# Strassen's seven products for four of eleven K-tile pairs of a down projection, in a float32 decoder layer

## The chip, the cores and the metric

The kernel runs on one core of a Trainium2 chip. The metric is device time in microseconds (us) of one execution, the median of several runs. TensorE (PE in the profile, PEld for its weight loads) multiplies matrices into PSUM banks; VectorE (DVE) and ScalarE (ACT) work elementwise and can read PSUM; GpSimd (POOL) works elementwise from SBUF; SyncE (SP) mostly issues DMA transfers. A tile lies on 128 partitions; "128x1024" is partitions by elements of each.

## The reference

A decoder layer in float32 on x of 256 tokens by 2048 features: two kinds of attention with one input and one output projection, then a channel mixer. Only the channel mixer is touched:

```python
h = rmsnorm(x, pre_ffn_g[l])
u = causal_dwconv(h @ w_up[l], conv_w[l], conv_b[l])      # 2048 -> 2 * 5632, width 3
gate, val = jnp.split(u, 2, axis=-1)
y = (jax.nn.gelu(gate, approximate=True) * val) @ w_down[l]   # 5632 -> 2048
x = x + rmsnorm(y, post_ffn_g[l])
```

## The kernel before

**Numbers.** Each float32 operand is split into a high part of a format that TensorE multiplies fast (fp32r in the profile) and a low part, the rest. A product is the sum of three matmuls: high by high, high by low, low by high. ScalarE makes the high part (a copy that rounds), VectorE the low part (operand minus high part). For weights these are the lines L111 and L114 (`w_split`), for activations L311 and L312 (`split`).

**Weights.** `w_load` (L68) lets SP's queue bring 512 KB of weights into a tile `raw` (128x1024); `raw` is a ring of five, so a load waits until the tile five loads earlier has been read by its low part. High and low parts, `whi` and `wlo`, are rings of five too.

**The channel mixer** runs in two halves of the 5632 features. In each half eleven steps g make two tiles each of `G`, the activated features: 22 tiles of 128 features by 256 tokens, each as high part (columns 0 to 255) and low part (256 to 511). One step multiplies the normalised input hT (16 K tiles, high and low) by 256 gate columns and 256 value columns of w_up (`proj_T4`, L283 for high weights, L289 for low ones). Each result goes through `conv`: ScalarE copies the cross term out of PSUM (`cs`, L879), VectorE adds (`u`, L880), GpSimd multiplies by the token scales (L881), ScalarE makes the first tap (L883), VectorE the other two (L885, L887). Then gate times value (L958) and the split into `G`. Banks of PSUM come from two tags, "acc" and "att", four of each; steps g take turns between them, from "acc" in both halves.

**The down projection** of a half follows its eleven steps: G (22 K tiles) by w_down, in passes of 512 output columns (n = 0 to 3). A pass has eleven pairs of K tiles; a pair is one load of two K tiles by 512 columns, and 2 K tiles x 2 token tiles x 3 = 12 matmuls of 128x512 (`mm3`, L308), added up in two PSUM banks. In half 0 ScalarE copies the result to `y_sb`; in half 1 `down` adds PSUM to `y_sb` (L972), squares and sums for the norm (L973) and multiplies by the gain (GpSimd, with the gain tile `gbf`). Half 1's last pass (n = 3) is written out separately: it keeps the last parts in the memory of hT (`rest`), and finishes with the residual `x_sb` and the output transfers.

**Order.** TensorE's order is the program's. The other engines' orders come from a scheduler, except where the program fixes them (the first gate step up to `order.__exit__`, and the finish). What an engine does next is fixed when the kernel is built; at run time each instruction waits for its operands.

## Time and profile before

| | |
|---|---|
| median of 3 runs | 1077.66 us (1077.61 to 1078.52) |
| profiled execution: span | 1076.3 us |
| TensorE busy | 1064.1 us (99%) |
| VectorE, ScalarE, GpSimd busy | 744.6, 611.2, 219.7 us (69%, 57%, 20%) |
| read from memory | 199.58 MB, 187 GB/s over the span |
| up projection, half 0, to its last up matmul | until 584.90 us |
| down projection, half 0 | 584.90 to 704.58 |
| up projection, half 1 | 704.58 to 947.02 |
| down projection, half 1, to its last pass's wait | 947.02 to 1067.66 |

The span is that of one profiled execution, 1.4 us under the median of the runs. The stage limits are ends of pieces in the chain of waits (the chain of work that ended last, followed back). In rows of the profile, "L308" is a line of the kernel, "x528" a count, and what follows "|" is the busy time of a group, the mean of one in ns, and the idle time before them with what ended it. Where a row begins with two numbers, they are its start in us and its length. A row of a table of windows has a window, its length, and for PE, PEld, DVE, ACT and POOL the busy time with the count in brackets; then the granted TensorE clock (1.00 is full), the DMA engines' busy share, and GB/s.

### The profile page before, as it was taken

Reading aid. Unit: us, or ns where it says so; the run is one execution under the profiler, and the core shown is the slowest. Engines: PE = TensorE matmul, PEld = TensorE weight load, DVE = VectorE, ACT = ScalarE, POOL = GpSimd, SP = SyncE. Lnnn points to the kernel's source line nnn. Section 1 sums busy time; section 2 is a strip of 40 time slices with the busy share of each in tenths; the row PEclk is TensorE's granted clock in tenths of the full one; section 3 lists DMA queues with packets and bytes.
Section 4 is the critical chain, followed back from the end, with each engine's and each line's share of the span. In section 5 each row is a group of like instructions: output and inputs, shape, how many; then the busy total and the mean of one; then the engine's idle time right before and its main releaser. Section 6 shows DMA issues by size and latency. Waiting matters only on the chain.

```text
span 1076.3 us, 16248 instructions
## 1 busy us (share of the span) xinstructions
PE 1064.1 (99%) x5986; PEld 926.8 (86%) x5986; DVE 744.6 (69%) x1200; ACT 611.2 (57%) x1060; POOL 219.7 (20%) x252
## 2 busy tenths in 40 slices
PE   9999999999999999999999999999999999999996
PEld 7889988887889888888888888888888888888886
DVE  5988877887577876777777444457777777765563
ACT  6766766666556765655555443446555555644450
POOL 4243343332022121212122000002121221201111
PEclk9999999999999999999999999999999999999999
DMA  8635556555873666656565666666565666666652
GB/s 282 209 119 176 183 155 210 158 161 157 298 235 105 216 214 193 189 186 197 186 190 193 196 197 193 195 193 190 184 197 188 189 193 193 193 192 197 193 167 79
DMA packets 164970, 202.88 MB, mean 188 GB/s; under 512 B 6780, under 2 KB 130972, under 8 KB 164380
## 3 DMA queue, kind: packets, MB, share of 16 engines
q1 hardware_dynamic: 164176, 201.27, 59.0%
q8 instruction: 47, 0.77, 0.3%
q10 hardware_dynamic: 716, 0.58, 0.2%
q14 instruction: 31, 0.25, 0.1%
HBM read 199.58 MB, written 2.11 MB: 187 GB/s over the span
## 4 chain that ended last, share of the span: by engine, by line
PE 93%; DVE 2%; DMA 1%; POOL 1%; ACT 1%; issue 1%; SPq 0%; DVEq 0%; POOLq 0%; ACTq 0%
PE bank_acc L308 34%; PE bank_acc L283 16%; PE bank_att L283 14%; PE bank_acc L289 8%; PE bank_att L289 7%; PE bank_acc L252 5%; PE bank_acc L257 3%; DVE wlo L114 1%; PE bank_att L474 1%; PE bank_att L509 1%; PE bank_acc L914 1%; PE bank_acc L910 0%; PE bank_att L220 0%; POOL scr L441 0%; PE bank_att L533 0%
## 5 line engine op out<-in xcount | busy, mean ns | idle before, releaser
L114 DVE TENSOR_TENSOR wlo<-raw,whi 128x1024 fp32r<-128x1024 f32 (+3 forms) x357 | 438.4, 1236 | 239.6 <-ACT whi L111 235.6
L111 ACT CAST whi<-raw 128x1024 fp32r<-128x1024 f32 (+3 forms) x356 | 363.8, 1035 | 258.6 <-issue 123.7
L308 PE MATMUL bank_acc<-whi,G 128*128 128x512 f32 (+1 forms) x724 | 214.4, 378 | 0.0
L881 POOL TENSOR_TENSOR u<-u,rowf 128x256 f32<-128x256 f32 x88 | 95.7, 1108 | 496.9 <-DVE u L880 493.4
L283 PE MATMUL bank_acc<-hT,whi 128*128 128x512 f32 x736 | 173.3, 390 | 0.0
L283 PEld LDWEIGHTS bank_acc<-hT,whi 128*128 128x128 f32 x736 | 136.4, 188 | 27.4
L308 PEld LDWEIGHTS bank_acc<-whi,G 128*128 128x128 f32 x724 | 133.7, 188 | 25.5
L283 PE MATMUL bank_att<-hT,whi 128*128 128x512 f32 x640 | 150.6, 390 | 0.0
L283 PEld LDWEIGHTS bank_att<-hT,whi 128*128 128x128 f32 x640 | 118.7, 188 | 23.9
L308 PE MATMUL bank_acc<-wlo,G 128*128 128x512 f32 (+1 forms) x362 | 137.0, 379 | 0.0
L289 PEld LDWEIGHTS bank_acc<-hT,wlo 128*128 128x128 f32 x736 | 89.3, 188 | 2.0
L289 PE MATMUL bank_acc<-hT,wlo 128*128 128x256 f32 x736 | 89.8, 279 | 0.0
L252 PE MATMUL bank_acc<-hT,whi 128*128 128x512 f32 x352 | 89.2, 396 | 0.0
L308 PE MATMUL bank_acc<-whi,oT 128*128 128x512 f32 (+1 forms) x272 | 82.5, 380 | 0.0
L308 PEld LDWEIGHTS bank_acc<-wlo,G 128*128 128x128 f32 x362 | 68.1, 188 | 12.9
L289 PEld LDWEIGHTS bank_att<-hT,wlo 128*128 128x128 f32 x640 | 77.6, 188 | 1.7
L289 PE MATMUL bank_att<-hT,wlo 128*128 128x256 f32 x640 | 77.9, 279 | 0.0
L252 PEld LDWEIGHTS bank_acc<-hT,whi 128*128 128x128 f32 x352 | 63.0, 188 | 11.3
L308 PEld LDWEIGHTS bank_acc<-whi,oT 128*128 128x128 f32 x272 | 50.2, 188 | 9.3
L308 PE MATMUL bank_acc<-wlo,oT 128*128 128x512 f32 (+1 forms) x136 | 51.3, 377 | 0.0
L308 PE MATMUL bank_acc<-whi,hT 128*128 128x384 f32 (+1 forms) x192 | 47.5, 324 | 0.0
L257 PE MATMUL bank_acc<-hT,wlo 128*128 128x256 f32 x352 | 47.5, 282 | 0.0
(204 smaller groups left out, 1140.4 us busy)
## 6 DMA issues: line engine op xcount, KB each, us to landing
raw<-in_w_up_dram SPq DMA_DIRECT2D x176, 512.0 KB, 3.7
raw<-in_w_down_dram SPq DMA_DIRECT2D x88, 512.0 KB, 4.6
raw<-in_w_in_dram SPq DMA_DIRECT2D x51, 512.0 KB, 3.5
raw<-in_w_out_dram SPq DMA_DIRECT2D x32, 512.0 KB, 4.7
raw<-in_w_in_dram SPq DMA_DIRECT2D x16, 384.0 KB, 3.3
cb<-c_dram SPq DMA_DIRECT2D x8, 256.0 KB, 3.5
x_sb<-in_x_dram SPq DMA_DIRECT2D x2, 1024.0 KB
raw<-in_w_in_dram SPq DMA_DIRECT2D x5, 408.0 KB, 3.2
```

Source lines behind the costliest of these rows:

```text
L111: i1 = act.copy(hi[:, cs], raw[:, cs])
L114: i2 = dve.tensor_tensor(lo[:, cs], raw[:, cs], hi[:, cs].bitcast(F32), op=ALU.subtract)
L252: pe.matmul(b, parts[u][0][:, a, m * P:(m + 1) * P], hT[:, kt, :], start=(kt == 0), stop=(kt == KT - 1))
L257: pe.matmul(b[:, 256:512], parts[u][1][:, a, m * P:(m + 1) * P], hT[:, (v + u) * 4 + a, 0:256], start=False, stop=False)
L283: pe.matmul(b, parts[u][0][:, a, m * P:(m + 1) * P], hT[:, kt, :], start=(kt == 0), stop=(kt == KT - 1))
L289: pe.matmul(b[:, 256:512], parts[u][1][:, a, m * P:(m + 1) * P], hT[:, kt, 0:256], start=False, stop=False)
L308: pe.matmul(b, a, r[:, cols], start=(first and i == 0), stop=(last and i == 2))
L474: pe.matmul(sb[e][:, cs], a[r, t * P:(t + 1) * P], b[r, 0:nk], start=(n == 0), stop=(n == 2))
L509: pe.transpose(pb[:, i * P:(i + 1) * P], p[:, e, c:c + P], ident)
L881: pool.tensor_tensor(u[:, 2:258], u[:, 2:258], rowf, op=ALU.mult)
L914: pe.matmul(v(b), hi[:, ms], v(hT[:, kt, :]), start=(t == 0 and kt == 0), stop=False)
```

## The change

Two K tiles by 1024 output columns of w_down are seen as 2x2 blocks (K tile by half of the columns), and two token tiles by these two K tiles of G as 2x2 blocks as well. Their product needs eight block products; Strassen's scheme, in Winograd's form, needs seven, of sums and differences of blocks. The constant `FAST = (0, 2, 4, 6)` names the pairs for which this is done; the other seven pairs of a pass stay plain. What moves with it:

- **Passes.** Half 0's four passes of 512 columns become two of 1024, both with fast pairs (`fast_pass`). Half 1's passes n = 0 and 1 become one fast pass; n = 2 and n = 3 stay as they were. Here a pair is two loads of one K tile by 1024 columns (rows of 4 KB in place of two of 2 KB). A plain pair of a fast pass is 24 matmuls of 128x512, a fast pair 7 x 3 = 21.
- **Weight side.** A fast pair's seven products take as weights: the left half of the first raw tile (high and low part of 512 columns), two tiles of differences, `tb` (four subtractions of 512 columns, L983, L984, L987 and L989, and two splits of 1024), and the whole second raw tile. So per fast pair VectorE makes four subtractions and four low parts, ScalarE four high parts; a plain pair of two raw tiles has two of each. The four subtractions hang together: the third needs the first and the fourth the third. The fourth matmul product on uses the second tile of differences.
- **Where tb lies.** In half 0 it takes the memory tag "gbc", before the gain tile does; in half 1 the tag "hT", the memory of hT.
- **Token side.** For the eight fast pairs of the two halves, `token_sums` makes four sums and differences of 128x128 blocks on VectorE, and their split, as soon as the two tiles of G are there. They are kept in `sums`, which takes the memory tag "x", that of `x_sb`.
- **x.** `x_sb` is therefore written to memory (two transfers of 1 MB issued by ScalarE after the squares of the first gate step) and read back as `x_back` in the last pass.
- **PSUM.** All eight banks are held through a fast pass: four sums for the early products (m1, m5, m7, m6), added after the last fast pair (`add_early`), and four for output blocks, added at the end of the pass (`add_late`). In half 0 early banks are of tag "att", late ones of "acc"; in half 1 the other way round. The steps g of half 1 start with "att" now.
- **Adds.** In half 0 the copies out of PSUM become eight adds and one copy per pass; in half 1 a fast pass has eight adds and one copy ahead of the four `down`.

```diff
--- before.py
+++ after.py
+FAST = (0, 2, 4, 6)
...
+            for t in range(2):
+                act.dma_start(x_dram[t * P:(t + 1) * P, :], x_sb[:, t, :])
...
+        def token_sums(into, y0, y1):
+            s = fp.tile([P, 4, P], F32, tag="cst", name="s")
+            a11, a21 = y0[:, 0:P], y0[:, P:256]
+            a12, a22 = y1[:, 0:P], y1[:, P:256]
+            dve.tensor_tensor(s[:, 0, :], a21, a22, op=ALU.add)
+            dve.tensor_tensor(s[:, 2, :], a11, a21, op=ALU.subtract)
+            dve.tensor_tensor(s[:, 1, :], s[:, 0, :], a11, op=ALU.subtract)
+            dve.tensor_tensor(s[:, 3, :], a12, s[:, 1, :], op=ALU.subtract)
+            split(into[:, 0:512], into[:, 512:UNIT], s.rearrange("p k c -> p (k c)"))
+        def product(b, lh, ll, rhs, cols, first, last):
+            hi, lo = rhs
+            for i, (a, r) in enumerate(((lh, hi), (lh, lo), (ll, hi))):
+                pe.matmul(b, a, r[:, cols], start=(first and i == 0), stop=(last and i == 2))
+        def fast_pass(G, sums, k00, c0, tb, early, late, add_early, add_late):
...
+            m1, m5, m7, m6 = early
+            p2, p3, p4, p22 = late
+            for u in range(pairs):
+                k = 2 * u
+                ra, rb = (w_load(w_rows(w_down, k00 + k + a, 1, c0, UNIT), 1, UNIT)[0]
+                          for a in range(2))
+                if u in FAST:
+                    i = FAST.index(u)
+                    one, end = i == 0, i == len(FAST) - 1
+                    def s_of(j):
+                        return (sums[:, i, j * P:(j + 1) * P],
+                                sums[:, i, 512 + j * P:512 + (j + 1) * P])
+                    b11 = parts(ra[:, left], 512)
+                    t13, t24 = tb[:, 0, :], tb[:, 1, :]
+                    dve.tensor_tensor(t13[:, left], ra[:, right], ra[:, left], op=ALU.subtract)
+                    dve.tensor_tensor(t13[:, right], rb[:, right], ra[:, right],
+                                      op=ALU.subtract)
+                    f13 = parts(t13, UNIT)
+                    dve.tensor_tensor(t24[:, left], rb[:, right], t13[:, left],
+                                      op=ALU.subtract)
+                    dve.tensor_tensor(t24[:, right], rb[:, left], t24[:, left],
+                                      op=ALU.subtract)
+                    f24 = parts(t24, UNIT)
+                    b2 = parts(rb, UNIT)
+                    product(m1, *of(k, 0), b11, left, one, end)
+                    product(m5, *s_of(0), f13, left, one, end)
+                    product(m7, *s_of(2), f13, right, one, end)
+                    product(m6, *s_of(1), f24, left, one, end)
+                    product(p4, *of(k + 1, 1), f24, right, one, False)
+                    product(p2, *of(k + 1, 0), b2, left, one, False)
+                    product(p3, *s_of(3), b2, right, one, False)
+                    if end:
+                        add_early()
+                    continue
+                b = [parts(ra, UNIT), parts(rb, UNIT)]
+                blocks = ((p2, 0, left), (p3, 0, right), (p4, 1, left), (p22, 1, right))
+                end = u == pairs - 1
+                order2 = ([(a, x) for x in blocks for a in range(2)] if end else
+                          [(a, x) for a in range(2) for x in blocks])
+                for a, (bk, t, cols) in order2:
+                    product(bk, *of(k + a, t), b[a], cols,
+                            bk is p22 and u == plain[0] and a == 0, end and a == 1)
+                    if end and a == 1:
+                        add_late(t, 1 if cols is right else 0, bk)
...
-                alt = g % 2
+                alt = (g + half) % 2
...
+                if g in FAST:
+                    if sums is None:
+                        sums = main.tile([P, len(FAST), UNIT], F32R, tag="x", name="sums")
+                    token_sums(sums[:, FAST.index(g), :], *ys)
...
-                if half == 0:
-                    act.copy(ys, b[:, cs])
-                else:
-                    dve.tensor_tensor(ys, b[:, cs], ys, op=ALU.add)
-                    act.activation(junk[:, cs], ys, AF.Square, accum_out=ysq[t][:, i:i + 1])
-                    pool.tensor_tensor(ys if into is None else into, ys,
-                                       gbf[:, n * 512:(n + 1) * 512][:, cs], op=ALU.mult)
+                dve.tensor_tensor(ys, b[:, cs], ys, op=ALU.add)
+                act.activation(junk[:, cs], ys, AF.Square, accum_out=ysq[t][:, i:i + 1])
+                pool.tensor_tensor(ys if into is None else into, ys,
+                                   gbf[:, n * 512:(n + 1) * 512][:, cs], op=ALU.mult)
...
-            for n in range(3 + (half == 0)):
+            tags = ("acc", "att") if half else ("att", "acc")
+            tb = (main.tile([P, 4, UNIT * 2], F32, tag="hT", name="tb")[:, 0:2, 0:UNIT] if half else
+                  fp.tile([P, 2, UNIT], F32, tag="gbc", name="tb"))
+            for n in range(0, 2 if half else 4, 2):
+                early, late = ([bank(tag) for _ in range(4)] for tag in tags)
...
+                def add_early():
+                    m1, m5, m7, m6 = early
+                    if half == 0:
+                        act.copy(y_of(0, 0), m1)
+                        dve.tensor_tensor(y_of(0, 1), m6, y_of(0, 0), op=ALU.add)
+                        dve.tensor_tensor(y_of(1, 0), m7, y_of(0, 1), op=ALU.add)
+                        dve.tensor_tensor(y_of(0, 1), m5, y_of(0, 1), op=ALU.add)
+                        dve.tensor_tensor(y_of(1, 1), m5, y_of(1, 0), op=ALU.add)
+                        return
...
+                fast_pass(G, sums, half * FHALF, n * 512, tb, early, late, add_early, add_late)
+            for n in range(2, 2 + half):
...
-                                     x_sb[:, t, cs], op0=ALU.mult, op1=ALU.add)
+                                     x_back[:, t, cs], op0=ALU.mult, op1=ALU.add)
...
+        rest = main.tile([P, KT, 512], F32R, tag="hT", name="rest")
+        x_back = main.tile([P, 2, D], F32, tag="x", name="x_back")
...
+            if u in (1, 2):
+                sp.dma_start(x_back[:, u - 1, :], x_dram[(u - 1) * P:u * P, :])
```

Three places of the order, as the built programs have it. A row is a line, an operation, and the tile written <- the tiles read; "x3" is three of the kind in a row; a number behind a name marks one tile among several of that name. In the program after, the lines of `conv` are L881 to L889, those of the weight splits in a fast pass L312 and L313, and the product of gate and value L1040.

VectorE, from the last value step of half 1 into its down projection, before. The first two rows are the additions with which the last `conv` begins; `G_7331` and `G_7332` are the last two tiles of G.

```order
L880 TENSOR_TENSOR u_3940<-bank_acc,cs 128x256
L880 TENSOR_TENSOR u_3941<-bank_acc,cs 128x256
L114 TENSOR_TENSOR wlo<-raw,whi 128x1024
L885 SCALAR_TENSOR_TENSOR yv<-u_3940,cw,yv 128x256
L885 SCALAR_TENSOR_TENSOR yv<-u_3941,cw,yv 128x256
L887 SCALAR_TENSOR_TENSOR yv<-u_3940,cw,yv 128x256
L887 SCALAR_TENSOR_TENSOR yv<-u_3941,cw,yv 128x256
L958 TENSOR_TENSOR yv<-yv,yg 128x256 x2
L114 TENSOR_TENSOR wlo<-raw,whi 128x1024
L312 TENSOR_TENSOR G_7331<-yv,G_7331 128x256
L312 TENSOR_TENSOR G_7332<-yv,G_7332 128x256
L114 TENSOR_TENSOR wlo<-raw,whi 128x1024 x9
```

The low parts `wlo` of the down projection's first pairs stand between and behind the convolution's operations, and nothing but `conv` and raw tiles is read there.

The same place after the change.

```order
L983 TENSOR_TENSOR tb<-raw 128x512
L882 TENSOR_TENSOR u_3941<-bank_att,cs 128x256
L882 TENSOR_TENSOR u_3942<-bank_att,cs 128x256
L984 TENSOR_TENSOR tb<-raw 128x512
L987 TENSOR_TENSOR tb<-raw,tb 128x512
L887 SCALAR_TENSOR_TENSOR yv<-u_3941,cw,yv 128x256
L887 SCALAR_TENSOR_TENSOR yv<-u_3942,cw,yv 128x256
L889 SCALAR_TENSOR_TENSOR yv<-u_3941,cw,yv 128x256
L889 SCALAR_TENSOR_TENSOR yv<-u_3942,cw,yv 128x256
L1040 TENSOR_TENSOR yv<-yv,yg 128x256 x2
L313 TENSOR_TENSOR wlo<-tb,whi 128x1024
```

The first difference stands ahead of the two additions; the second and third between the additions and the taps; the first low part of `tb` behind the product of gate and value. What comes next on VectorE:

```order
L313 TENSOR_TENSOR G_7454<-yv,G_7454 128x256
L313 TENSOR_TENSOR G_7455<-yv,G_7455 128x256
L989 TENSOR_TENSOR tb<-raw,tb 128x512
L983 TENSOR_TENSOR tb<-raw 128x512
L984 TENSOR_TENSOR tb<-raw 128x512
L313 TENSOR_TENSOR wlo<-tb,whi 128x1024
L313 TENSOR_TENSOR wlo<-raw,whi 128x1024 x3
L313 TENSOR_TENSOR wlo<-raw,whi 128x512
L313 TENSOR_TENSOR wlo<-tb,whi 128x1024
```

The fourth difference stands behind G's low parts, and two differences of the second fast pair (pair 2) stand ahead of the low part of the first pair's second `tb` tile.

ScalarE at the same place, after the change.

```order
L881 COPY cs<-bank_att 128x256 x2
L885 ACTIVATE yv<-u_3941,cw 128x256
L885 ACTIVATE yv<-u_3942,cw 128x256
L312 CAST whi<-tb 128x1024
L312 CAST G_7454<-yv 128x256
L312 CAST G_7455<-yv 128x256
L312 CAST whi<-tb 128x1024
L312 CAST whi<-raw 128x1024 x3
```

The high part of the first `tb` tile stands behind the two first taps of the last `conv`, and that of the second behind the casts of G. Before the change one `whi<-raw` cast stood between the taps and the casts of G, and ten behind them.

VectorE inside half 0's first fast pass, after the change: the first row is the first difference of the third fast pair (pair 4), the third the low parts of the plain pair 3, and the second `L983` that of pair 6.

```order
L983 TENSOR_TENSOR tb<-raw 128x512
L984 TENSOR_TENSOR tb<-raw 128x512
L313 TENSOR_TENSOR wlo<-raw,whi 128x1024 x2
L313 TENSOR_TENSOR wlo<-raw,whi 128x512
L987 TENSOR_TENSOR tb<-raw,tb 128x512
L313 TENSOR_TENSOR wlo<-tb,whi 128x1024
L989 TENSOR_TENSOR tb<-raw,tb 128x512
L983 TENSOR_TENSOR tb<-raw 128x512
L313 TENSOR_TENSOR wlo<-tb,whi 128x1024
L313 TENSOR_TENSOR wlo<-raw,whi 128x1024
L984 TENSOR_TENSOR tb<-raw 128x512
L987 TENSOR_TENSOR tb<-raw,tb 128x512
```

Ahead of a `L984`, which reads a pair's second raw tile, stand the low parts and differences of the pairs before it.

More of the change, by code (lines that the diff above doesn't have):

```diff
@@ L743, in hybrid_layer @@
         hT = hT2
+        x_dram = tc.dram_tile([S, D], F32, name="x_dram")
         dffn, rmix = [], []
@@ new lines, in product, with of, parts @@
+        def product(b, lh, ll, rhs, cols, first, last):
[3 more added lines that the diff above has]
+        def fast_pass(G, sums, k00, c0, tb, early, late, add_early, add_late):
+            left, right = slice(0, 512), slice(512, UNIT)
+            pairs = FHALF // 2
+            plain = [u for u in range(pairs) if u not in FAST]
+            def of(k, t):
+                return G[k][:, t * P:(t + 1) * P], G[k][:, 256 + t * P:256 + (t + 1) * P]
+            def parts(src, n):
+                hi, lo = w_parts(n)
+                split(hi, lo, src)
+                return hi, lo
+            m1, m5, m7, m6 = early
[42 more added lines that the diff above has]
+                        add_late(t, 1 if cols is right else 0, bk)
@@ L936, in hybrid_layer @@
             G = [fp.tile([P, 512], F32R, tag="G", bufs=FHALF, name=f"G{j}") for j in range(FHALF)]
+            sums = None
             for g in range(FHALF // 2):
                 c0 = (half * (FHALF // 2) + g) * 256
-                alt = g % 2
+                alt = (g + half) % 2
                 if half == 0 and g == 0:
@@ L947, in hybrid_layer @@
                     proj_T4(w_up, c0, bg)
[L948 removed]
+                gates, ys = [], []
                 for m in range(2):
@@ L960, in hybrid_layer @@
                     split(gt[:, 0:256], gt[:, 256:512], y)
+                    ys.append(y)
+                if g in FAST:
+                    if sums is None:
+                        sums = main.tile([P, len(FAST), UNIT], F32R, tag="x", name="sums")
+                    token_sums(sums[:, FAST.index(g), :], *ys)
             if half == 1:
-                rest = main.tile([P, KT, 512], F32R, tag="hT", name="rest")
                 gbf = fp.tile([P, D], F32, tag="gbc", name="gbc_ffn")
```

18 lines of the change are left out of this document (17 added, 1 removed).

## The prediction

> **What bounds the kernel now.** I read the page's busy times first, then the chain of waits, then the two stretches in which the down projection runs, each as one piece of that chain.
>
> ```profile
> span 1076.3 us, 16248 instructions
> ...
> PE 1064.1 (99%) x5986; PEld 926.8 (86%) x5986; DVE 744.6 (69%) x1200; ACT 611.2 (57%) x1060; POOL 219.7 (20%) x252
> ...
> PE 93%; DVE 2%; DMA 1%; POOL 1%; ACT 1%; issue 1%; SPq 0%; DVEq 0%; POOLq 0%; ACTq 0%
> ```
>
> TensorE carries 93% of the chain, so a matmul that goes away is time that goes away, as long as what feeds TensorE keeps up.
>
> ```profile
> 581.25 3.65 PE bank_acc L283 x16
> 584.90 119.68 PE bank_acc L308 x528
> 704.58 3.63 PE bank_acc L283 x16
> ...
> 943.37 3.65 PE bank_acc L283 x16
> 947.02 120.64 PE bank_acc L308 x594
> ```
>
> The first half's down projection is 528 matmuls without a gap: 119.68 / 528 = 0.2267 us each. The row after it starts as it ends. The second half's starts at 947.02, the same instant at which the last up matmul's piece ends; I call this instant T below.
>
> ```profile
> 592.00:704.00 112.00, 112.00 (x496) 92.75 (x495) 51.69 (x44) 46.64 (x49) 0.00 (x0) 1.00 0.63 196
> 720.00:940.00 220.00, 220.00 (x1279) 194.43 (x1278) 162.75 (x240) 126.97 (x201) 44.39 (x40) 1.00 0.61 191
> ```
>
> Columns are PE, PEld, DVE, ACT, POOL, granted clock, DMA share, GB/s. In the down projection VectorE is busy 51.69 of 112 us (46%); in the up projection 162.75 of 220 (74%). There is room on VectorE in the very stretch where the change puts work.
>
> **What is removed.** A fast pair needs 21 matmuls of 128x512 instead of 24. Four pairs in two passes of half 0 and in one of half 1 make 12 times 3 = 36 matmuls: 36 x 0.2267 = 8.2 us, 5.4 in half 0 and 2.7 in half 1. The four ScalarE evictions per pass of half 0 were hidden and are worth nothing.
>
> **The feed in the steady part.** Per fast pair VectorE now makes four subtractions and one low part of 512 columns and three low parts of 1024; ScalarE makes the high parts.
>
> ```profile
> 7.72 0.69 DVE L114 TENSOR_TENSOR wlo<-raw,whi 128x512 fp32r<-128x512 f32 x1
> 372.11 2.35 DVE L114 TENSOR_TENSOR wlo<-raw,whi 128x1024 fp32r<-128x1024 f32 x2
> 577.63 1.99 ACT L111 CAST whi<-raw 128x1024 fp32r<-128x1024 f32 x2
> ```
>
> One 1024-wide low part takes 1.22 us and two in a row 2.35, so the next starts after 1.13; the 512-wide one takes 0.69, some 0.60 in a row by the same overlap. A fast pair costs 5 x 0.60 + 3 x 1.13 = 6.4 us of VectorE against 21 x 0.2267 = 4.76 of TensorE: alone it would be bound by VectorE. But a plain pair follows each: 2 x 1.13 = 2.3 against 24 x 0.2267 = 5.44. Together VectorE needs 8.7 of 10.2 us; ScalarE, with six casts of 0.95 or less, under 5.6. So it is hidden, with 1.5 us to spare per two pairs.
>
> That spare is what a late load may eat. Five raw buffers are a ring, so the load for a fast pair's first raw tile is asked for when the second raw tile of the plain pair two pairs earlier has been read. By the order quoted ahead, VectorE reaches the subtraction that needs the new tile after one 512-wide low part, one subtraction, one 1024-wide low part and one subtraction: 0.60 + 0.60 + 1.13 + 0.60 = 2.9 us. A load that lands L us after its issue makes VectorE wait L - 2.9, of which 1.5 is spare; TensorE loses L - 4.4. It happens at pairs 4 and 6 of both passes of half 0, four times.
>
> ```profile
> DMA to landing us min/median/max: 4.1/4.6/4.9
> ...
> DMA to landing us min/median/max: 3.3/3.7/4.8
> ...
> gbc_ffn<-in_post_ffn_g_dram SPq DMA_DIRECT2D x1, 1024.0 KB, 5.2
> ```
>
> The first row is the raw tiles between 600 and 700 us (rows of 2 KB), the second those between 720 and 940 (1 KB). The changed loads have rows of 4 KB and no row here shows them. The low end is 3.7, which costs nothing; the high end is the 5.2 of a load with twice the bytes and 8 KB rows: 4 x 0.8 = 3.2. I take 4.6, the same tensor and the same bytes: 4 x 0.2 = **0.8 us**. [...]
>
> **The start of half 1's down projection.** This is the term that decides. In half 0 the tile of differences, tb, has its own memory. In half 1 it lies where hT lies, and the last up matmul reads hT: the first difference can be made at T and not before. In the order it stands ahead of the two additions with which the last value part's convolution begins, and the rest of tb's chain is mixed into that convolution. How the convolution runs today:
>
> ```profile
> 946.83 0.66 ACT L879 COPY cs<-bank_acc 128x256 f32<-128x256 f32 x2 [0.49 <-PE bank_acc L283]
> ...
> 948.69 0.60 ACT L883 ACTIVATE yv<-u,cw 128x256 f32<-128x256 f32 x1 [0.26 <-POOL u L881]
> 950.27 0.60 ACT L883 ACTIVATE yv<-u,cw 128x256 f32<-128x256 f32 x1 [0.98 <-POOL u L881]
> ...
> 947.52 0.75 DVE L880 TENSOR_TENSOR u<-bank_acc,cs 128x256 f32<-128x256 f32 x2
> ...
> 952.10 0.75 DVE L958 TENSOR_TENSOR yv<-yv,yg 128x256 f32<-128x256 f32 x2
> 952.77 1.22 DVE L114 TENSOR_TENSOR wlo<-raw,whi 128x1024 fp32r<-128x1024 f32 x1
> 953.90 0.75 DVE L312 TENSOR_TENSOR G<-yv,G 128x256 fp32r<-128x256 f32 x2
> ...
> 948.01 2.22 POOL L881 TENSOR_TENSOR u<-u,rowf 128x256 f32<-128x256 f32 x2 [8.80 <-DVE u L880]
> ...
> L111 ACT CAST whi<-raw 128x1024 fp32r<-128x1024 f32 x42 | 44.3, 1054 | 61.1 <-PE bank_acc L308 60.1 <-issue 1.0
> ```
>
> The additions start at T + 0.50, the second activation ends at 950.87 = T + 3.85, the two products end at 952.85 = T + 5.83. Now the same with the change:
> - A matmul's result lags its start, so the first difference begins about T + 0.16; with its 0.6 the additions move from T + 0.50 to about T + 0.77, and all of the convolution by 0.27. The second activation ends at T + 4.1.
> - Behind it on ScalarE stands the high part of the first two differences: 1.05 us, to T + 5.2.
> - VectorE ends the two products at T + 6.1 and only then makes the low part: 1.22 us, to T + 7.25. TensorE has done the first product (3 matmuls, T + 0.68) and one matmul of the second; the other needs this low part.
> - VectorE then makes the two low parts of G (0.75, to T + 7.95) and the last difference (0.69, to T + 8.6). ScalarE: its high part, to T + 9.65. VectorE: the next pair's first two differences until about T + 9.8, then the low part of the second pair of differences, 1.22, to T + 11.0.
> - TensorE has 11 matmuls of this fast pair left then (two of the fourth product, nine of the last three): 2.5 us, to T + 13.5. Without waits it would have been T + 4.76.
>
> The loss is **8.7 us**. With every instruction at its in-a-row pitch and no shift it is 8.2, with none overlapped 9.1. Before the change nothing here waited: the weights were split ahead of T, and the late G is the last of 22 tiles read. Later pairs of this pass find their parts ready, since VectorE goes on while TensorE waits.
>
> **Small edits.** Token sums, eight times: four 128x128 operations (nearest row below, 0.28), a low part of 0.69 and a cast. That is 1.8 us more in a group of 22 us with 16.3 busy: hidden.
>
> ```profile
> 354.57 0.28 DVE L202 TENSOR_SCALAR diag<-ident,rffn 128x128 f32<-128x128 f32 x1
> ...
> L972 DVE TENSOR_TENSOR y_sb<-bank_acc,y_sb 128x512 f32<-128x512 f32 x7 | 4.5, 684 | 8.7 <-PE bank_acc L308 8.7
> ```
>
> Eight adds out of PSUM per fast pass in half 0 are 5.5 us; a pass is 4 x 4.76 + 7 x 5.44 = 57 us with 4 x 6.4 + 7 x 2.3 = 41.7 of VectorE: hidden under the plain pairs at its end; eight more than today in half 1 the same. Parking x writes 2 MB near 357 us, where the DMA share is 0.61 at 191 GB/s: the idle 0.39 is worth some 120 GB/s, so it takes about 17 us beside the weights. The first token sums want that memory about then, and behind that wait on ScalarE stand the next evictions and casts: 0 to 2 us. I take 0, since ScalarE is busy only 58% there. Reading x back is 2 MB in a stretch with a share of 0.53: nothing.
>
> **Sum.** -8.2 + 8.7 + 0.8 = +1.3 us on the profiled execution (span 1076.3, beside a median of 1077.66; the 1.4 between them stays). Prediction **1079.0 us**: the gain is spent on one start-up. What this kernel can tell from no change is 0.2%, or 2.2 us: 1075.5 to 1079.8 is "same".
>
> **Rivals.**
> *Slower: the raw ring starves VectorE in half 0.* Place: the first difference of pairs 4 and 6. Price: 4 x (L - 4.4). With the 0.5 of the other terms it leaves "same" from L = 4.85 on; at 5.2 the time is 1077.66 + 0.5 + 3.2 = 1081.4, at 6 it is 1084.6. For it: today's maxima of 4.9, and loads come four in 10.2 us, 6% faster than today. Against: the median of 4.6, and 37% of the DMA engines' time is idle. [...] Chance 0.40.
> *Faster: the start-up is hidden.* If only the parts of hT that tb covers had to be free (k tiles 0, 1, 4 and 5, last read in the low matmuls some 5.5 us before T), the differences would be made ahead of the convolution: -8.2 + 0.8, so 1070.3. Against: in the order the first difference stands behind everything of the gate part, which is done long before T, and its second piece behind T's additions. Chance 0.08.
>
> The forecast has 0.52. Range: low 1076.0 (all costs at their low ends give 1077.7; the rest leans to the hidden start-up), high 1084.5 (the ring at L = 6). Faster 0.08, same 0.52, slower 0.40.
>
> **What would show it.** Half 0's down projection, 119.7 us now, should take 114.3 to 117.5; more, with gaps at the fast pairs behind VectorE and loads, is the ring. At the start of half 1's TensorE should stand idle 8 to 9 us in four pieces, waiting first for ScalarE's cast of tb, then VectorE's low part, and the same again. If there is no such gap the forecast is wrong by its largest term; if gaps show in the up projection, token sums or the parking were not hidden.

## The result

The changed kernel takes 1088.22 us (median of 4, 1086.94 to 1089.64) where the kernel before takes 1077.95: a ratio of 1.0094, 95% interval 1.0079 to 1.0108. It is slower by 10.3 us; 1079.0 was predicted, with a range up to 1084.5.

The page of the changed kernel: span, busy times, and the chain of waits by engine.

```profile
span 1085.4 us, 16365 instructions
PE 1060.9 (98%) x5950; PEld 919.6 (85%) x5950; DVE 818.7 (75%) x1336; ACT 630.8 (58%) x1087; POOL 219.7 (20%) x252
PE 83%; DVE 7%; DMA 5%; issue 2%; ACT 2%; POOL 1%; SPq 0%; DVEq 0%; POOLq 0%; ACTq 0%
```

There are 36 matmuls fewer (5950 against 5986 records), and yet TensorE's share of the chain has fallen from 93% to 83%, with VectorE and DMA in its place. The chain in order of time shows where:

```profile
601.40 5.81 DMA raw<-in_w_down_dram
...
650.52 6.41 DMA raw<-in_w_down_dram
...
662.36 6.25 DMA raw<-in_w_down_dram
...
944.48 3.67 PE bank_att L284 x16
...
958.55 1.22 PE bank_acc L951 x2
959.77 9.37 PE bank_att L951 x33
```

In half 0's down projection the chain runs through loads of w_down. At the start of half 1's it leaves TensorE from 948.15 to 958.55, and the 35 matmuls after that take 10.59 us, 0.30 each, where matmuls of 128x512 take 0.2267 when nothing waits.

From the first matmul of a stage to the first of the next (for the last: to the end of its last matmul), in us of the profiled executions. Every kernel of the experiments is in the table, its ratio against runs of the kernel before that were made beside it (medians 1077.5 to 1078.2); the up projection of half 1 between the two stages took 242.4 in all of them.

| kernel | half 0's down projection | half 1's | time, median | ratio to before (95%) |
|---|---|---|---|---|
| before | 119.68 | 120.79 | 1077.95 | |
| changed | 120.46 | 128.89 | 1088.22 | 1.0094 (1.0079 to 1.0108) |
| changed, second measurement | 122.87 | 128.44 | 1087.96 | 1.0092 (1.0079 to 1.0106) |
| fast pairs in half 0 alone | 123.02 | 120.79 | 1080.43 | 1.0019 (1.0009 to 1.0028) |
| tb in own memory in half 1 | 121.34 | 118.08 | 1077.97 | 0.9997 (0.9988 to 1.0007) |
| order pinned in half 0 | 114.46 | 127.26 | 1079.35 | 1.0011 (1.0001 to 1.0021) |
| pairs spaced in half 0 | 114.24 | 126.53 | 1079.26 | 1.0006 (0.9995 to 1.0016) |
| sixth raw tile in half 0 | 116.04 | 128.77 | 1082.23 | 1.0036 (1.0022 to 1.0050) |
| no fast pair | 119.68 | 120.79 | 1078.23 | 1.0002 (0.9993 to 1.0012) |
| plain pair first in half 1 | 121.40 | 121.10 | 1081.94 | 1.0028 (1.0017 to 1.0040) |
| useless matmuls in half 1's gap | 120.79 | 128.15 | 1087.25 | 1.0086 (1.0070 to 1.0103) |
| own memory and spaced pairs | 114.24 | 118.07 | 1070.56 | 0.9925 (0.9913 to 0.9938) |

504 matmuls at 0.2267 us are 114.26, so the gain of 5.4 us is whole in half 0 where nothing waits (114.24), and the changed kernel lost 6.2 there. In half 1, 118.07 is what is left without a wait; the changed kernel lost 10.8.

**Half 0.** Waits in the changed kernel between 585 and 705 us, the ones for loads (us in total, times, longest):

```profile
DVE tb L983 <- DMA raw<-in_w_down_dram: 12.7, 5, 3.7
...
DVE tb L984 <- DMA raw<-in_w_down_dram: 1.2, 2, 0.8
```

The first difference of a fast pair waits 2.5 us on average, up to 3.7, for its raw tile. One such wait, and what TensorE got of it:

```profile
607.30 0.69 DVE L983 TENSOR_TENSOR tb<-raw 128x512 f32<-128x512 f32 x1 [2.99 <-DMA raw<-in_w_down_dram]
...
609.19 0.50 PE L951 MATMUL bank_att<-wlo,sums 128*128 128x512 f32 x1 [1.10 <-DVE wlo L313]
```

The difference is that of pair 6. In VectorE's order it stands ahead of the low part of pair 4's second tile of differences, and that is what TensorE waits for.

**Half 1.** TensorE's timeline there (start, length, and in brackets the idle time before with what ended it), VectorE's and ScalarE's instructions that it waits for, and windows of the same stretch, with the granted clock behind the five engines' busy times (three of them divide the 10.24 us at 0.50, from 953.36 to 963.60; the first is as long, ahead of them):

```profile
947.97 0.39 PE L951 MATMUL bank_acc<-whi,G 128*128 128x512 f32 x1
...
952.57 0.49 PE L951 MATMUL bank_acc<-whi,sums 128*128 128x512 f32 x1 [3.77 <-ACT whi L312]
954.94 0.80 PE L951 MATMUL bank_acc<-wlo,sums 128*128 128x512 f32 x1 [1.88 <-DVE wlo L313]
...
958.55 0.79 PE L951 MATMUL bank_acc<-wlo,sums 128*128 128x512 f32 x1 [0.47 <-DVE wlo L313]
...
963.41 0.48 PE L951 MATMUL bank_att<-whi,G 128*128 128x512 f32 x1
```

```profile
948.17 0.69 DVE L983 TENSOR_TENSOR tb<-raw 128x512 f32<-128x512 f32 x1 [6.66 <-PE bank_att L284]
...
953.68 1.21 DVE L313 TENSOR_TENSOR wlo<-tb,whi 128x1024 fp32r<-128x1024 f32 x1
...
957.29 1.21 DVE L313 TENSOR_TENSOR wlo<-tb,whi 128x1024 fp32r<-128x1024 f32 x1
...
951.49 1.03 ACT L312 CAST whi<-tb 128x1024 fp32r<-128x1024 f32 x1
```

```profile
949.94:953.36 3.42, 0.49 (x1) 0.19 (x1) 3.42 (x8) 2.14 (x3) 1.01 (x1) 1.00 0.40 144
953.36:956.77 3.41, 1.83 (x4) 1.51 (x5) 3.41 (x8) 1.32 (x3) 0.00 (x0) 0.50 0.02 10
956.77:960.18 3.41, 2.94 (x7) 1.63 (x6) 3.41 (x4) 3.41 (x5) 0.00 (x0) 0.50 0.00 0
960.18:963.60 3.42, 3.42 (x10) 2.65 (x9) 3.42 (x5) 1.47 (x2) 0.00 (x0) 0.50 0.74 192
```

The first fast pair's 21 matmuls run from 947.97 to 963.41, 15.44 us in place of 4.76: 10.7 are lost. The waits are those that were forecast, in the same order, but three in place of four, 6.1 us of idle time in place of 8 to 9. The granted clock falls to 0.50 behind the first of them; the slowed matmuls cover the wait for the second cast, and the pair's last 11 matmuls take 4.86 us where 2.49 would do.

### The profile page after: what moved, and what is told of

Read it like the earlier page. It is cut to its first block, busy times and chain, and to the rows that moved or that the text cites. A ratio compares the mean times of both kernels' runs of the same rounds, so it can differ in the third digit from the quotient of the medians.

```text
span 1085.4 us, 16365 instructions
## 1 busy us (share of the span) xinstructions
PE 1060.9 (98%) x5950; PEld 919.6 (85%) x5950; DVE 818.7 (75%) x1336; ACT 630.8 (58%) x1087; POOL 219.7 (20%) x252
## 4 chain that ended last, share of the span: by engine, by line
PE 83%; DVE 7%; DMA 5%; issue 2%; ACT 2%; POOL 1%; SPq 0%; DVEq 0%; POOLq 0%; ACTq 0%
PE bank_acc L309 18%; PE bank_att L284 15%; PE bank_acc L284 14%; PE bank_att L290 8%; PE bank_acc L290 7%; PE bank_acc L253 5%; PE bank_att L951 5%; PE bank_acc L951 4%; DMA raw<-in_w_down_dram 3%; PE bank_acc L258 3%; DVE wlo L313 2%; DVE wlo L115 1%; PE bank_att L475 1%; PE bank_att L510 1%; PE bank_acc L916 1%
## 5 line engine op out<-in xcount | busy, mean ns | idle before, releaser
L115 DVE TENSOR_TENSOR wlo<-raw,whi 128x1024 fp32r<-128x1024 f32 (+3 forms) x291 | 358.4, 1241 | 136.9 <-ACT whi L112 132.7
L112 ACT CAST whi<-raw 128x1024 fp32r<-128x1024 f32 (+3 forms) x290 | 294.5, 1031 | 151.8 <-issue 91.9
L284 PE MATMUL bank_acc<-hT,whi 128*128 128x512 f32 x672 | 158.2, 390 | 0.0
L253 PE MATMUL bank_acc<-hT,whi 128*128 128x512 f32 x352 | 89.2, 396 | 0.0
L312 ACT CAST whi<-raw 128x1024 fp32r<-128x1024 f32 (+1 forms) x66 | 62.4, 973 | 41.9 <-PE bank_acc L951 14.8
L951 PE MATMUL bank_acc<-whi,G 128*128 128x512 f32 x264 | 84.7, 389 | 0.0
L290 PE MATMUL bank_acc<-hT,wlo 128*128 128x256 f32 x672 | 82.1, 279 | 0.0
L313 DVE TENSOR_TENSOR wlo<-raw,whi 128x1024 fp32r<-128x1024 f32 (+1 forms) x66 | 73.2, 1132 | 9.3 <-ACT whi L312 9.3
L951 PEld LDWEIGHTS bank_acc<-whi,G 128*128 128x128 f32 x264 | 49.6, 188 | 10.3
L951 PE MATMUL bank_acc<-wlo,G 128*128 128x512 f32 x132 | 52.2, 395 | 2.9 <-DVE wlo L313 2.7
L309 PE MATMUL bank_acc<-whi,G 128*128 128x512 f32 (+1 forms) x196 | 51.8, 350 | 0.0
```

Source lines behind the costliest of these rows:

```text
L112: i1 = act.copy(hi[:, cs], raw[:, cs])
L115: i2 = dve.tensor_tensor(lo[:, cs], raw[:, cs], hi[:, cs].bitcast(F32), op=ALU.subtract)
L253: pe.matmul(b, parts[u][0][:, a, m * P:(m + 1) * P], hT[:, kt, :], start=(kt == 0), stop=(kt == KT - 1))
L284: pe.matmul(b, parts[u][0][:, a, m * P:(m + 1) * P], hT[:, kt, :], start=(kt == 0), stop=(kt == KT - 1))
L290: pe.matmul(b[:, 256:512], parts[u][1][:, a, m * P:(m + 1) * P], hT[:, kt, 0:256], start=False, stop=False)
L309: pe.matmul(b, a, r[:, cols], start=(first and i == 0), stop=(last and i == 2))
```

## The experiments

All kernels compute the whole result. A diff shows the core of an edit to the changed kernel.

**Fast pairs in half 0 alone.**

```diff
-                if g in FAST:
+                if half == 0 and g in FAST:
...
-            for n in range(0, 2 if half else 4, 2):
+            for n in range(0, 0 if half else 4, 2):
...
-            for n in range(2, 2 + half):
+            for n in range(0, 3 * half):
```

> Fast pairs in half 0 alone; half 1's passes are plain again, x is still parked. Theory: the changed kernel lost in two places that have nothing to do with each other, 6.2 us in half 0 (its down projection took 120.5 us where 36 fewer matmuls would give 114.3) and 10.8 us in half 1 (128.7 where 117.9 was due). Then half 1's down projection is back at 120.6 us, half 0's stays at 120.5, and the time is 1088.2 - 8.1 = 1080.1 us (1078.5 to 1081.5). Rival, one common cause (the parking, the sums, or the other banks slow everything a little): half 1 stays above 123 us and the time above 1083.

Measured: 1080.43 us, half 1 back at 120.79. Its chain has half 1's down projection in one piece again, and half 0's gaps are still there, the longest at 609 us:

```profile
949.97 120.64 PE bank_acc L309 x594
```

```profile
609.24 0.50 PE L951 MATMUL bank_att<-wlo,sums 128*128 128x512 f32 x1 [1.96 <-DVE wlo L313]
```

The two losses are separate. Here half 0 took 123.0, more than in the changed kernel's profile (a reason is in the last section).

**The differences of half 1 in own memory.**

```diff
-            tb = (main.tile([P, 4, UNIT * 2], F32, tag="hT", name="tb")[:, 0:2, 0:UNIT] if half else
-                  fp.tile([P, 2, UNIT], F32, tag="gbc", name="tb"))
+            tb = fp.tile([P, 2, UNIT], F32, tag="gbc", name="tb")
...
-                gbf = fp.tile([P, D], F32, tag="gbc", name="gbc_ffn")
-                sp.dma_start(gbf, post_ffn_g[0].partition_broadcast(P))
+                gbf = [fp.tile([P, 256], F32, tag=("yg", "yv")[j // 4], bufs=4, name=f"gb{j}")
+                       for j in range(8)]
```

> The differences of half 1 get memory of their own, the one they have in half 0; the gain tile goes, in eight pieces, where the convolution's gate and value tiles were. All else as changed. Theory: the stall at the start of half 1 is the wait for the last reader of hT, so the first pair's differences and parts are made before the last up matmul, TensorE starts without a gap, its granted clock stays at 1.00, half 1's down projection takes 117.9 to 118.5 us in place of 128.7, and the time is 1088.2 - 10.5 = 1077.7 us (1076 to 1079.5). Rival: the chain of a fast pair that stands first is mixed into the last convolution and is late wherever its memory lies: a gap of 4 us or more stays and the time is above 1082.

Measured: 1077.97 us; half 1 takes 118.08. VectorE makes the first pair's low parts and the second pair's differences ahead of the last up matmul (which ends at 948.68), and TensorE goes on without a gap:

```profile
942.82 2.45 DVE L313 TENSOR_TENSOR wlo<-tb,whi 128x1024 fp32r<-128x1024 f32 x2
945.19 0.69 DVE L987 TENSOR_TENSOR tb<-raw 128x512 f32<-128x512 f32 x1
```

```profile
945.03 3.65 PE bank_att L284 x16
948.68 2.72 PE bank_acc L951 x12
```

With the wait for hT gone the scheduler has put the whole chain ahead of the last convolution's additions, and half 1's 10.8 us are gone, the clock's part included. The wait for hT, with the order that came of it, was the cause.

**VectorE's and ScalarE's order pinned in half 0** (pairs 3 to 6 of each pass, differences first):

```diff
+            def pin(i):
+                if k00 == 0 and 3 <= u <= 6:
+                    tc.keep_in_program_order(i)
...
-                    b11 = parts(ra[:, left], 512)
+                    b11 = high(ra[:, left], 512)
...
+                        pin(dve.tensor_tensor(out, p, q, op=ALU.subtract))
+                    b11 = low(b11)
```

> Half 0 alone: pairs 3 to 6 of both fast passes have VectorE's and ScalarE's work pinned in the order of the pairs, with the four differences of a pair in a row ahead of its low parts; five raw tiles as before. Theory of the order: VectorE loses time because a difference of pair 6 stands ahead of parts of pair 4 that are ready and that TensorE needs; a load that lands after 5.2 to 6.4 us then holds these up. With the pins half 0's down projection takes 115 to 117 us in place of 120.5, the time is 1083 to 1085. Theory of the ring (my prediction's rival as it was written: five raw tiles are too few): the loads are asked for as late as before, half 0 stays at 119 to 121.5 us and the time at 1087 to 1089.

Measured: 1079.35 us, half 0 at 114.46, better than expected; the time is 3.7 us under its range. (Half 1's work is written in this order too, unpinned; 127.26 there, which is 1.6 of the 3.7.) The same five raw tiles and the same work, and the waits for loads on the differences have gone from 12.7 + 1.2 to 4.5 us:

```profile
DVE tb L999 <- DMA raw<-in_w_down_dram: 4.5, 4, 1.5
```

**Half 0's fast pairs spaced.**

```diff
-FAST = (0, 2, 4, 6)
+FASTS = ((0, 3, 6, 9), (0, 2, 4, 6))
```

> Half 0's fast pairs are 0, 3, 6 and 9 instead of 0, 2, 4 and 6, so that two plain pairs follow each; half 1 as changed. Same matmuls, same VectorE and ScalarE work, same loads. Theory (a late load has 1.5 us of spare per two pairs; with one more plain pair the spare is 1.5 + 3.1 = 4.6): no gap is left in half 0, it takes 114.3 to 115 us, and the time is 1082 to 1083. Rival, VectorE's throughput over the whole pass or slower loads of 4 KB rows: spacing changes no sum of work, half 0 stays above 118 and the time above 1086.

Measured: 1079.26 us, half 0 at 114.24, no gap. Neither VectorE's throughput nor the row size was the limit: with the same sum of work everything is hidden. Nor do the loads land sooner here; their median between 590 and 680 us is 6.1 us, and 5.0 in the changed kernel:

```profile
DMA to landing us min/median/max: 3.6/6.1/7.8
```

The time is 3 us under the expectation, 2.4 of it in half 1, whose code was not touched. Its gap is the same (3.77), but the clock is back sooner:

```profile
948.89:952.30 3.41, 3.05 (x6) 1.78 (x6) 3.41 (x7) 1.80 (x2) 0.00 (x0) 0.50 0.00 0
952.30:955.71 3.41, 2.95 (x13) 2.36 (x13) 3.41 (x4) 3.41 (x5) 0.00 (x0) 1.00 0.18 31
```

```profile
952.86 0.50 PE L951 MATMUL bank_acc<-wlo,sums 128*128 128x512 f32 x1 [0.46 <-DVE wlo L313]
...
955.49 0.39 PE L951 MATMUL bank_att<-whi,G 128*128 128x512 f32 x1
```

In both kernels the last 11 matmuls begin 10.6 us after the stage's first; they take 2.63 us here and 4.86 in the changed kernel. That difference of 2.2 us is the clock; 126.53 - 118.07 = 8.5 us is the wait alone.

**A sixth raw tile in half 0.**

```diff
+        if sixth:
+            raw = extra[0].tile([P, UNIT], F32, tag="raw6", name="raw")
...
+                                 sixth=k00 == 0 and (k + a) % 6 == 5)[0]
...
-            c = fp.tile([P, 256], F32, tag="cs", bufs=3, name="cs")
+            c = fp.tile([P, 256], F32, tag="cs", bufs=2, name="cs")
...
-        last = fp.tile([P, 256], F32, tag="last", name="last")
+        last = fp.tile([P, 256], F32, tag="cst", name="last")
```

> Half 0 as changed, fast pairs 0, 2, 4 and 6, the scheduler's order, but with a sixth raw tile for the fast passes of half 0 (room from the last output piece, which moves into other memory, and one of three cross-term tiles). Theory of the ring: a load is asked for one tile earlier and is there in time; half 0's down projection falls from 120.5-123 us to 114.5-116 and the time to 1082-1083.5. Theory of the order: the difference of a later fast pair still stands ahead of ready work, and its load is asked for only a little earlier; half 0 stays at 118 to 121 us and the time at 1086 to 1088.

Measured: 1082.23 us, half 0 at 116.04. This is what the theory of the ring expected of half 0 (to 0.04), and not what I had come to expect of the order after the two runs before. Differences (L990 and L991 here) wait less for loads:

```profile
  DVE tb L990: 3.9, 3
  DVE tb L991: 3.5, 4
...
DMA to landing us min/median/max: 3.6/4.5/6.7
```

Of the 1.8 us above 114.24 some 1.1 is a slower pace of the matmuls in half 0: the plain pairs at a pass's end, 105 matmuls in one piece of the chain, take 24.03 us here and 23.80 in the changed kernel (0.2289 against 0.2267 each, times 504). So little of the loss is left. The cause of that pace stays open.

**No fast pair**, but passes of 1024 columns and loads with rows of 4 KB, and x parked:

```diff
-FAST = (0, 2, 4, 6)
+FAST = ()
...
-                        dve.tensor_tensor(y_of(t, c), b, y_of(t, c), op=ALU.add)
+                        act.copy(y_of(t, c), b)
```

> No fast pair at all: the passes of 1024 columns with loads of one K tile by 1024 columns (rows of 4 KB) stay, every pair is plain, no sums and no differences; x is still parked and read back, half 0's results are copied out as before. It measures the loads of 4 KB rows where they are asked for evenly. If such rows are slow in themselves, the median from issue to landing in half 0 is 5.2 us or more, as in the changed kernel; if the changed kernel's loads were late because they came in bursts, it is 4.6 or less. The time is that of the kernel before either way, 1077.5 to 1079, since 24 matmuls a pair hide it; more would mean that the parking costs something.

Measured: 1078.23 us, both stages as before. Loads of w_down between 590 and 680 us, from issue to landing (the traces have the landing of about a third of them), without fast pairs, then in the changed kernel (the expectation had 5.2 for it):

```profile
DMA to landing us min/median/max: 3.6/4.6/4.9
```

```profile
DMA to landing us min/median/max: 3.5/5.0/9.5
```

Rows of 4 KB landed in 4.6 us here, where they are asked for evenly: the median of the kernel before. No cost of the parking is seen.

**A plain pair first in half 1.**

```diff
-FAST = (0, 2, 4, 6)
+FASTS = ((0, 2, 4, 6), (1, 3, 5, 7))
```

> Half 1's fast pairs are 1, 3, 5 and 7 instead of 0, 2, 4 and 6; its differences stay in hT's memory, half 0 stays as changed. The first, plain pair is 24 matmuls, 5.4 us of cover for a chain that ended some 10 us late. Theory: gaps of about 3 us in all remain in the first fast pair, in short pieces, so that the granted clock stays at 1.00; half 1's down projection takes 120.5 to 122 us in place of 128.9 and the time is 1080 to 1082. Rival (the half-speed stretch of some 10 us belongs to this place or to VectorE's load, not to the idle time before it): the clock falls here too, half 1 stays above 124 and the time above 1083.

Measured: 1081.94 us, half 1 at 121.10, as expected. The first difference still waits for hT, but 24 matmuls cover most of its chain. Three short gaps are left, of 0.44 us and these two, and the clock stays at 1.00:

```profile
957.89 0.50 PE L951 MATMUL bank_acc<-whi,sums 128*128 128x512 f32 x1 [0.90 <-ACT whi L312]
959.15 0.50 PE L951 MATMUL bank_acc<-wlo,sums 128*128 128x512 f32 x1 [0.77 <-DVE wlo L313]
```

```profile
953.00:960.00 7.00, 4.89 (x20) 3.17 (x19) 7.00 (x12) 4.08 (x7) 0.00 (x0) 1.00 0.12 47
```

**Useless matmuls in the gap**, with the changed kernel beside it.

```diff
+                    for _ in range(17 if first else 0):
+                        pe.matmul(p2, of(k, 0)[0], b11[0], start=True, stop=True)
...
+                for _ in range(9 if between and i == 1 else 0):
+                    pe.matmul(*between, start=True, stop=True)
```

> The changed kernel with 26 useless matmuls at the start of half 1's down projection: 17 behind the first product and 9 behind the first matmul of the second, into a bank whose content is overwritten later. They fill the two long waits of TensorE there (3.8 and 1.9 us) and nothing else; the result is the same. Theory (of the 10.7 us lost there 8.3 are the wait for VectorE's and ScalarE's parts and 2.4 the halved clock that follows the idle time): the clock stays at 1.00, the parts come at the same times, the first fast pair ends 2.4 us sooner, half 1's down projection takes 126.5 us in place of 128.9. Rival (the clock falls there for another reason, or useless matmuls slow the parts): 128.9 us or more.

> The changed kernel itself, on the chip and in the rounds of the run with the useless matmuls, to compare the two: half 1's down projection 128.9 us; half 0's, which hangs on when loads land, 120 to 123 us; the time 1087 to 1090 us.

Measured: 1087.25 us with them and 1087.96 without; half 1 at 128.15 and 128.44. I had expected 126.5, and that failed. The two long gaps were filled, at a clock of 1.00. But TensorE, now quicker, then ran into two short gaps that the slow clock had hidden, and behind these the clock fell after all, to 0.50 for 3.41 us:

```profile
957.97 0.50 PE L953 MATMUL bank_acc<-whi,sums 128*128 128x512 f32 x1 [0.91 <-ACT whi L312]
959.23 0.76 PE L953 MATMUL bank_acc<-wlo,sums 128*128 128x512 f32 x1 [0.76 <-DVE wlo L313]
...
963.45 0.40 PE L953 MATMUL bank_att<-whi,G 128*128 128x512 f32 x1
```

```profile
955.89:959.30 3.41, 1.75 (x7) 0.84 (x6) 3.41 (x7) 2.43 (x3) 0.00 (x0) 1.00 0.02 5
959.30:962.71 3.41, 3.41 (x8) 2.71 (x9) 3.41 (x4) 2.95 (x4) 0.00 (x0) 0.50 0.38 86
```

So the run does not take the clock's part away, but it gives a third size of it. Here too the last 11 matmuls begin 10.6 us after the stage's first, so the useless matmuls did not slow the parts; they take 4.22 us. From one and the same instant these 11 matmuls take 4.86, 4.22 or 2.63 us, as the clock is at 0.50 for all, most or none of them, where 2.49 is the pace at full clock. And 126.5 + 1.7 (4.22 - 2.49) = 128.2 is what was measured.

**Both cures**: own memory for half 1's differences, pairs 0, 3, 6 and 9 in both halves.

> Both cures together: the differences of half 1 in memory of their own, and fast pairs 0, 3, 6 and 9 in both halves. If the two losses are separate and these were their causes, half 0's down projection takes 114.3 us (114.2 with the spacing alone) and half 1's 118 (118.1 with own memory alone), against 119.7 and 120.8 of the kernel before: 1077.8 - 5.4 - 2.7 = 1069.7 us (1069 to 1072). Rival: the losses move elsewhere when both are cured (VectorE's extra work shows up in the up projections, or loads): above 1074.

Measured: 1070.56 us (5 runs, 1069.08 to 1070.89), faster than before by 0.75% (0.62 to 0.87). Its chain in half 1 has TensorE from the last up matmul to the last pass in pieces that join:

```profile
938.92 3.65 PE bank_att L284 x16
942.57 2.72 PE bank_acc L951 x12
945.29 12.92 PE bank_att L951 x57
```

The stages gain 5.4 and 2.7 us; this is the change as it could have been. (The median gains 7.6 of these 8.2, and the profiled span 7.2: its down projection of half 0 begins 1.0 us later than before, at 585.73.)

## Why the prediction was wrong

**What is removed** held to the hundredth: 119.68 - 114.24 = 5.44 and 120.79 - 118.07 = 2.72 us, 8.2 in all.

**Small edits** held: half 1's up projection takes 242.4 us with and without the token sums, the adds fit under the plain pairs (114.24 leaves no room for a gap), and the kernel with parking and wide passes alone measures 1.0002.

**The feed in the steady part: the term "4 x 0.2 = 0.8 us" failed.** It came to 6.2 us in the profiled execution. The mechanism was the one described, a raw ring that makes VectorE wait at the first difference of a fast pair, and the sign named for it came (120.46 us, with gaps behind VectorE and loads); the size was that of the rival. What was mis-sized is L, the landing time: I took the 4.6 of today's evenly spaced loads, since it was the same tensor and the same bytes. Evenly asked for, rows of 4 KB did land in 4.6 (the run without fast pairs). But a fast pair's work on VectorE frees raw tiles in groups, so loads are issued in groups (at 612.6, 613.8 and 614.4 us, for one). Two moments of the changed kernel's loads, one issued alone and two issued 0.6 us apart behind a third (a line with count and times of issue, then the landing):

```profile
L69 SPq DMA_DIRECT2D raw<-in_w_down_dram x1: 328/328/328, 610.3 to 610.3; - x1
...
DMA to landing us min/median/max: 3.5/3.5/3.5
```

```profile
L69 SPq DMA_DIRECT2D raw<-in_w_down_dram x2: 327/328/328, 613.8 to 614.4; - x2
...
DMA to landing us min/median/max: 6.5/6.8/7.1
```

The load issued alone took 3.5 us, the two in the group 6.5 and 7.1. The loads that cost TensorE time are the three of the chain above, each issued within 3 us of others: 5.81, 6.41 and 6.25 us. The first differences that read them (pair 6 of the first pass, pairs 4 and 6 of the second) wait 2.99, 3.66 and 2.75 us. The two other waits (1.75 and 1.54 us, pairs 0 and 2 of the second pass) leave TensorE no gap, and pair 4 of the first pass does not wait there. By my formula, L - 4.4, the three come to 5.3 us, and 6.2 was measured. So the formula was near, with three places in place of four, and L was the error. I had rows that speak of it (the maximum of 4.9, the 5.2 of a load of 1 MB, and the remark that the loads come 6% faster), and read them as a rate where they were a matter of when the loads are asked for. The chance of 0.40 for this rival was fair; the fault is that the forecast stood on the low side of a steep curve. (A slip beside it: by its own terms the rival leaves "same" from L = 4.81 on, not 4.85.)

A late landing alone was no loss: the spaced kernel's loads took longer, 6.1 us in the median against 5.0, but VectorE had more to spare there, and TensorE had no gap (114.24).

What exactly is to blame in half 0 has no single answer. A sixth tile, another order and wider spacing each take away most or all of the 6.2 us. What they share, as I read their waits, is that VectorE stands less at a load that was asked for late while work that TensorE needs is queued behind it. One more buffer took half 0 to 116.04 us; the pinned order shows that buffers were not the only way (114.46 with five). The step from rows of 2 KB (before) to 4 KB (no fast pair) made no difference to the landing time here, 4.6 us in the median for both.

**The start of half 1: 8.7 us was forecast, 10.7 came. The step that failed is the pace of the matmuls behind the wait.** The chain was right, and its instants nearly so: T + 4.4 for the first cast (T is 948.15, and 951.49 + 1.03 = 952.52; forecast 5.2), T + 6.7 for the low part (forecast 7.25), T + 10.35 for the second low part (forecast 11.0). Behind it stood the step "TensorE has 11 matmuls of this fast pair left then: 2.5 us", which took the pace of a busy TensorE. They took 4.86. At full clock the loss would be 10.7 - 2.4 = 8.3, and 8.5 is what the spaced kernel's stage has, where the clock was back in time. I had quoted a granted clock of 1.00 for the kernel before and took it for a constant; it was read where TensorE had no gap, busy for 112.00 of 112.00 us and 220.00 of 220.00. Behind the gap the changed kernel's trace has ten matmuls from 959.15 to 963.41 that take 0.426 us each, against 0.2267, at a granted clock of 0.50. The forecast contained a gap of 4 us (3.77 came) and left that term out.

**The sum** was -8.2 + 8.7 + 0.8 = +1.3; it came to -8.2 + 10.7 + 6.2 = +8.7 on a profiled execution that is 9.1 us longer (0.3 of the rest lies ahead of the down projection). The median moved by 10.3. Half 0's loss differs between executions, 120.5 to 123.0 us in the six profiles of kernels with the same half 0, and the execution profiled first is one of the two shorter ones of four; that the median differs for this reason is likely but not shown.

**The rival of the hidden start-up** is settled by the trace: the first difference starts at 948.17, at the end of the last up matmul, and VectorE had stood idle for it for 6.66 us.

## What to carry to other kernels

When a change takes work off the bound engine by putting it on the feeding engines, look first at the two places where the feed has no lead: the first unit of a stage (what memory does its first operand wait for?) and the ring that refills (does the new work free buffers in groups?). The changed kernel's page has TensorE at 98% and shows neither. And price a stall on TensorE with the matmuls behind it, not only with its own length: in the changed kernel 11 of them took 4.86 us in place of 2.49.

## What the runs showed of the hardware

**The clock behind gaps of TensorE.** In the run with half 0 alone the granted clock is 1.00 in the window with the gap of 1.96 us, and 0.50 in the next, from 610.06 to 613.40 us:

```profile
606.65:610.06 3.41, 1.45 (x7) 0.86 (x5) 2.70 (x3) 1.40 (x2) 0.00 (x0) 1.00 0.11 44
610.06:613.40 3.34, 3.34 (x9) 2.62 (x8) 3.34 (x5) 1.04 (x1) 0.00 (x0) 0.50 0.47 155
```

In the second measurement of the changed kernel TensorE has a gap of 1.92 us there; the matmuls from 610.54 to 613.53 take 0.43 us each, and the mean granted clock from 600 to 615 us is 0.89. These two took 123.02 and 122.87 us for the same half 0. The changed kernel, the one with useless matmuls and the one with a plain pair first have no such stretch there and took 120.46, 120.79 and 121.40.

How long the clock stayed low differs: 3.41 us with useless matmuls (959.30 to 962.71), 10.24 in the changed kernel (953.36 to 963.60). In the changed kernel's four windows TensorE was busy for 0.49, 1.83 and 2.94 us where 0.50 came next, and for all of 3.42 us in the last, behind which the clock was 1.00. The length of the gaps alone does not decide it: behind 0.91 and 0.76 us (useless matmuls) the clock was 0.50, behind 0.90 and 0.77 (plain pair first) it was 1.00. No run sets the gaps for this, so what decides it is not shown.

**The landing time of a load.** Loads of the same 512 KB in rows of 4 KB took 3.5 us (issued alone) and 7.1 us (in a group of three) in the changed kernel. Over half 0's down projection there, the loads of w_down whose landing is recorded took 4.6 us in the median where at most one other load was issued from 3 us before to 2 us after (9 loads), and 6.5 where two or more were (5 loads). In the kernel before all 14 had at most one such neighbour; their median is 4.6 us, the longest 5.2. It is not all: one of the 9 took 9.5 us (issued at 678.8, 1.2 us behind a load of 1 MB), one of the 5 only 4.3, and no run sets the spacing of the loads alone.
